# The up-projection of a gated MLP in Winograd form: weight sums added in place by DMAs, other signs and another product order, shifted activation tiles, and attention score products on all 128 rows

## The chip, the cores and the metric

The kernel runs on one core of one Trainium2 chip. The metric is the device time in microseconds (us) of one execution. TensorE is called PE here, VectorE DVE, ScalarE ACT, GpSimd POOL and SyncE SP; PEld is PE's loading of weights (the stationary operand of a matmul), which can run beside a matmul.

## The reference, cut to what matters

One decoder layer on a sequence of 512 tokens, 2048 wide: a mixer of three head groups, a cross-attention, and a gated MLP; all in float32. The change touches two places of it.

```
# the MLP's first half (D_FF = 5504 = 43 tiles of 128)
val, gate = split(h @ w_up, 2)                  # h 512x2048, w_up 2048x11008
g = conv_b + sum(conv_w[i] * shifted(gate, i))  # causal, width 3
out = (silu(g) * val) @ w_down
# groups A (12 heads) and B (8 heads) of the mixer, head width 64
logits = q @ k.T * 64**-0.5 + bias
```

## The kernel before

All activations lie transposed, features on the 128 partitions and tokens along the row. float32 products are made in PE's float32r form: each operand is split into a high part and a rest (`hi` by an ACT copy, `lo` by a DVE subtraction), and a product is three matmuls, high by high, high by low, low by high (`mm3`, lines 351 to 353). Weights come by SP's DMAs into `wraw` tiles (128x1024, 512 KB, five buffers), and are split half by half into `whi` and `wlo` (128x512, five buffers each): line 312 on ACT, line 313 on DVE. PE can so be at most five halves behind the splits.

**Scores (`attend`, lines 491 to 553).** For each of the 20 heads of groups A and B, `qs` holds the high part of the queries in 64 rows and their low part in the other 64, and `kh` holds the high part of the keys twice. So line 516, on 128 rows, gives both products with the high keys. Line 517 adds the high queries by the low keys `kl`, on 64 rows. A head has four such pairs of matmuls, 128, 256, 384 and 512 columns wide, 80 pairs in all. They are issued in the background, between the projection's 512-column products (lines 351 to 353 and 392 to 394), which keep PE filled.

**Sums of activations (`token_sums`, lines 1131 to 1158).** A product of 2x2 blocks is made with seven block products in place of eight. The two blocks of tokens are the first and last 256, the two blocks of outputs are the value and the gate columns of an output tile `f`, and the inner dimension goes in eight pairs of 128-row blocks. For each pair, seven sums or differences of activation blocks are made, split, and kept: 56 tiles `sum` (32 of them in the slots of `xhi` and `xlo`), 128x512, the high part in bytes 0 to 1023 of a row and the low part in bytes 1024 to 2047.

**The products (`up`, lines 1162 to 1235).** For each of the 43 tiles `f`, four weight blocks `b11, b12, b22, b21` are loaded. DVE makes four sums of them in 128x1024 tiles: `t1 = b12 - b11`, `t2 = b22 - t1`, `b22 - b12`, `t2 - b21` (line 1189). The products come in the order 1, 6, 5, 7, 4, 2, 3. Each is eight pairs by three matmuls of 256 columns, 24 in all, from two weight halves; a tile has 168 matmuls, the stage 7,224. Results are combined in PSUM or by DVE and ACT in 256-column pieces, then follow the convolution, the silu, and a store of the tile (`gd`, 256 KB).

A scheduler decides where in each engine's row of instructions a step stands; each engine then runs its row in order. SP's row holds the loads and the stores, POOL's row has nothing in this stage.

Of the kernel before, what the change touches and what calls it, by code (L numbers as in the profile page):

```python
# [40 lines left out]
FT = D_FF // P  # L41
FB = 4
HT = S // 2
# [2 lines left out]
FC = ((0, 5), (5, 10))  # L46
GX_SLOTS = 16
GB_SLOTS = 10
LEVELS = (64, 32, 16, 8, 4, 2, 1)
A_PATTERNS = ((128, 1), (512, 4), (2048, 16))  # L50
REL_BUCKETS = 32
# [5 lines left out]
WR = 5  # L57
# [153 lines left out]
class _Trunk:  # L211
# [77 lines left out]
        return self.gains[:, i * KT + k:i * KT + k + 1]  # L289

    def xslot(self, n=S):
        hi = self.xp.tile([P, n], F32R, name="xhi", tag="xhi", bufs=KT, padded_shape=[P, S])
        lo = self.xp.tile([P, n], F32R, name="xlo", tag="xlo", bufs=KT, padded_shape=[P, S])
        return hi, lo

    def split(self, src, n=S):
# [194 lines left out]
    def attend(self, qf, kf, e, vv, bias_of, head, mix):  # L491
        nc, ab = self.nc, self.ab
        a = slice(DH * e, DH * e + DH)
        o = slice(DH - DH * e, 2 * DH - DH * e)
# [5 lines left out]
        nc.scalar.activation(kh[o], kf[a], AF.Copy)  # L500
# [10 lines left out]
        def scores(t):  # L511
            n = P * (t + 1)
            sc = self.pst("S")
            tt = slice(t * P, n)
            with self.behind():
                nc.tensor.matmul(sc[:, :n], qs[:, tt], kh[:, :n], start=True, stop=False)
                nc.tensor.matmul(sc[:, :n], qs[a, tt], kl[a, :n], start=False, stop=True)
# [613 lines left out]
    def token_sums(self, i, pool, tmp):  # L1131

        nc = self.nc
        y = []
        for e in range(2):
            t = tmp.tile([P, S], F32, name="y%d" % e, tag="y%d" % e, bufs=2)
            nc.scalar.activation(t, self.x1[2 * i + e], AF.Copy, scale=self.gain(2, 2 * i + e))
            y.append(t)
        a11, a21 = y[0][:, :HT], y[0][:, HT:]
        a12, a22 = y[1][:, :HT], y[1][:, HT:]  # L1140
        s = [tmp.tile([P, HT], F32, name="s%d" % n, tag="s%d" % n, bufs=2) for n in range(1, 5)]
        src = {1: a11, 6: s[1], 5: s[0], 7: s[2], 4: a22, 2: a12, 3: s[3]}
        made = {5: (a21, a22, ALU.add), 6: (s[0], a11, ALU.subtract), 7: (a11, a21, ALU.subtract),
                3: (a12, s[1], ALU.subtract)}
        out = {}
        for n, j in enumerate((1, 5, 6, 7, 4, 2, 3)):
            if j in made:
                nc.vector.tensor_tensor(src[j], made[j][0], made[j][1], op=made[j][2])
            slot = 7 * i + n
            if slot < 2 * KT:  # L1150
                tag = ("xhi", "xlo")[slot % 2]
                t = self.xp.tile([P, S], F32R, name=tag, tag=tag, bufs=KT)
# [4 lines left out]
            out[j] = (t[:, :HT], t[:, HT:])  # L1157
        return out


# [1 line left out]
    def up(self):  # L1162
# [9 lines left out]
        def cw(i, f):  # L1172
            return self.conv[:, i * FT + f:i * FT + f + 1]

        def raw(u):
            t = self.wp.tile([P, 1024], F32, name="wraw", tag="wraw", bufs=WR)
            nc.sync.dma_start(out=t, in_=d["w_up"][u])
            return t

        def product(j, w, ps, start, stop):  # L1180
            for h in range(2):
                th, tl = self.split_weights(w[:, h * 512:(h + 1) * 512])
                for k in range(4):
                    i, c = 4 * h + k, slice(k * P, (k + 1) * P)
                    self.mm3(ps, th[:, c], tl[:, c], *self.sums[i][j], start and i == 0, stop and i == NP - 1,
                             more=True)

        def tt(out, a, b, op):
            nc.vector.tensor_tensor(out, a, b, op=op)

        def one(f):
            b11, b12, b22, b21 = [raw(4 * f + i) for i in range(4)]
            pa, pb = self.acc()[:, :HT], self.acc()[:, :HT]
            pc, pd = self.pst("C")[:, :HT], self.pst("D")[:, :HT]
            s1, u2, u3 = [fb.tile([P, HT], F32, name=n, tag=n, bufs=1) for n in ("s1", "u2", "u3")]
            val = fb.tile([P, S], F32, name="val", tag="val", bufs=1)
            gp = gps[f % 2]
            product(1, b11, pa, True, True)
            nc.scalar.activation(s1, pa, AF.Copy)
            t1 = fb.tile([P, 1024], F32, name="t1", tag="t1", bufs=1)  # L1200
            t2 = fb.tile([P, 1024], F32, name="t2", tag="t2", bufs=1)
            tt(t1, b12, b11, ALU.subtract)
            tt(t2, b22, t1, ALU.subtract)
            product(6, t2, pb, True, True)
            tt(u2, pb, s1, ALU.add)
            product(5, t1, pc, True, True)
            if f == 0:
                self.R = self.rms(self.sqs, S, self.con)
            tt(b12, b22, b12, ALU.subtract)
            product(7, b12, pb, False, True)  # L1210
            tt(u3, pb, s1, ALU.add)
            tt(gp[:, 2 + HT:], pc, u3, ALU.add)
            tt(t2, t2, b21, ALU.subtract)
            product(4, t2, pd, True, True)
            tt(val[:, hi], u3, pd, ALU.subtract)
            product(2, b21, pa, False, True)
            nc.scalar.activation(val[:, lo], pa, AF.Copy)
            product(3, b22, pc, False, True)
            tt(gp[:, 2:2 + HT], pc, u2, ALU.add)
            tt(gp[:, 2:], gp[:, 2:], self.R, ALU.mult)  # L1220
# [5 lines left out]
            tt(c, c, val, ALU.mult)  # L1226
            self.gd[f] = self.dr.tile([P, S], F32, name="gd%d" % f)
            nc.sync.dma_start(out=self.gd[f], in_=c)

        self.gd = {}  # L1230
        for f in range(FT):
            one(f)
        es.close()
        self.es_sx.close()
        self.es_fa.close()
# [141 lines left out]

# [13 lines left out]
```

## Time and profile before

| | |
|---|---|
| median of 3 runs | 2430.11 us (2429.5 to 2431.83) |
| the profiled execution | 2430.49 us; span 2428.7 us, so 1.8 us lie around it |
| granted TensorE clock, mean | 0.991 |
| busy, share of the span | PE 98%, PEld 88%, DVE 68%, ACT 47%, POOL 4% |
| 350 to 740 us (groups A and B) | PE 388.82 of 390 us, DVE 260.72, ACT 211.05 |
| 1100 to 1900 us (inside the MLP up stage) | PE 800.00 of 800 us, DVE 704.99, ACT 426.45, 118 GB/s |

The up stage begins at about 1058 us and ends at about 1937 us. In the timeline a row is one instruction: its start, its duration, engine, line, tiles written and read, shape, and in square brackets the idle time before it with what ended it. Matmuls are pipelined, so a row's duration overlaps the next; what PE takes for one is read as the distance of two starts. In the views of waits and of groups the time behind the bar is idle time in front of the instructions and what ended it.

### The profile page before, as it was taken

What the parts mean: (1) busy time and instruction counts of PE and PEld (TensorE: products, weight loads), DVE (VectorE), ACT (ScalarE), POOL (GpSimd) and SP (SyncE); (2) the same over time, 40 slices, a digit from 0 to 9 for tenths busy, and PEclk for the clock granted to TensorE, in tenths of its full rate; (3) what the DMA queues carried; (4) which work ended last, traced back from release to release, by engine and by line L of the source; (5) the groups of instructions that cost most, each with busy time, mean ns of one, the idle gap of its engine ahead of it and who ended that gap; (6) DMA issues with size and microseconds to landing.
All of it is one profiled execution on the core that took longest, in us unless ns stands there. A gap on an engine that the chain in (4) does not pass through costs nothing.

```text
span 2428.7 us, 37893 instructions
## 1 busy us (share of the span) xinstructions
PE 2379.8 (98%) x14514; PEld 2128.5 (88%) x14514; DVE 1660.4 (68%) x3112; ACT 1130.8 (47%) x2165; POOL 88.5 (4%) x91
## 2 busy tenths in 40 slices
PE   9999999999999999889999999999999899999997
PEld 8798987777778888779999999999999888888887
DVE  7726656556786365898888888888888743343336
ACT  6323345455564254665555555555555532232223
POOL 2000000000002000100000000000000000000003
PEclk9999999999999999989999999999999999999999
DMA  6432122222224343123333333333333443243332
GB/s 205 143 100 77 54 97 78 94 79 88 87 70 156 121 143 119 46 76 117 119 121 118 118 118 118 118 118 119 118 119 118 156 141 122 96 156 98 115 102 73
DMA packets 87458, 269.15 MB, mean 111 GB/s; under 512 B 9788, under 2 KB 14540, under 8 KB 87276
## 3 DMA queue, kind: packets, MB, share of 16 engines
q1 hardware_dynamic: 79504, 254.64, 32.5%
q10 hardware_dynamic: 7772, 12.09, 1.5%
q8 instruction: 114, 1.87, 0.3%
q14 instruction: 68, 0.56, 0.1%
HBM read 251.18 MB, written 19.45 MB: 111 GB/s over the span
## 4 chain that ended last, share of the span: by engine, by line
PE 94%; DVE 3%; ACT 1%; POOL 1%; DMA 0%; issue 0%; DVEq 0%; SPq 0%; POOLq 0%; ACTq 0%
PE acc L351 18%; PE acc L353 18%; PE acc L352 18%; PE psC L351 3%; PE psC L353 3%; PE psC L352 3%; PE acc L392 3%; PE acc L394 3%; PE acc L393 3%; PE psD L353 2%; PE psD L352 2%; PE psD L351 2%; PE psV L352 1%; PE psU L352 1%; PE psV L353 1%; PE psU L353 1%
## 5 line engine op out<-in xcount | busy, mean ns | idle before, releaser
L338 DVE TENSOR_TENSOR wlo<-wraw,whi 128x512 fp32r<-128x512 f32 (+2 forms) x496 | 335.8, 681 | 428.6 <-ACT whi L337 421.8
L337 ACT ACTIVATE whi<-wraw 128x512 fp32r<-128x512 f32 (+2 forms) x496 | 304.6, 617 | 655.1 <-PE acc L352 391.7
L351 PE MATMUL acc<-xhi,whi 128*128 128x512 f32 (+1 forms) x1518 | 555.3, 366 | 14.8 <-ACT xhi L1254 8.9
L353 PE MATMUL acc<-xhi,wlo 128*128 128x512 f32 (+1 forms) x1518 | 546.0, 360 | 0.0
L352 PE MATMUL acc<-xlo,whi 128*128 128x512 f32 (+1 forms) x1475 | 533.3, 362 | 0.0
L351 PEld LDWEIGHTS acc<-xhi,whi 128*128 128x128 f32 x1518 | 288.3, 190 | 59.0 <-ACT xhi L1254 9.1
L353 PEld LDWEIGHTS acc<-xhi,wlo 128*128 128x128 f32 x1518 | 288.4, 190 | 42.8 <-issue 0.8
L352 PEld LDWEIGHTS acc<-xlo,whi 128*128 128x128 f32 x1475 | 280.3, 190 | 39.6 <-issue 0.8
L312 ACT ACTIVATE whi<-wraw 128x512 fp32r<-128x512 f32 x344 | 216.7, 631 | 205.2 <-PE acc L352 68.5
L313 DVE TENSOR_TENSOR wlo<-wraw,whi 128x512 fp32r<-128x512 f32 x344 | 232.6, 687 | 37.4 <-ACT whi L312 33.0
L312 ACT ACTIVATE whi<-t 128x512 fp32r<-128x512 f32 x258 | 162.7, 632 | 165.1 <-PE acc L352 98.5
L313 DVE TENSOR_TENSOR wlo<-t,whi 128x512 fp32r<-128x512 f32 x258 | 173.6, 688 | 43.4 <-ACT whi L312 43.1
L351 PE MATMUL acc<-sum,whi 128*128 128x256 f32 x559 | 158.7, 284 | 0.9 <-ACT sum L1155 0.9
L352 PE MATMUL acc<-sum,whi 128*128 128x256 f32 x559 | 158.7, 284 | 0.5 <-DVE sum L1156 0.5
L353 PE MATMUL acc<-sum,wlo 128*128 128x256 f32 x559 | 158.5, 284 | 0.0
L352 PE MATMUL acc<-xhi,whi 128*128 128x256 f32 x430 | 122.1, 284 | 0.0
L392 PE MATMUL acc<-whi,xhi 128*128 128x384 f32 (+2 forms) x320 | 114.8, 359 | 0.6 <-ACT xhi L304 0.5
L394 PE MATMUL acc<-whi,xlo 128*128 128x384 f32 (+2 forms) x320 | 111.9, 350 | 0.5 <-DVE xlo L305 0.4
L393 PE MATMUL acc<-wlo,xhi 128*128 128x384 f32 (+2 forms) x320 | 111.8, 350 | 0.0
L353 PE MATMUL acc<-xlo,wlo 128*128 128x256 f32 x387 | 109.8, 284 | 0.0
L351 PE MATMUL acc<-xlo,whi 128*128 128x256 f32 x387 | 109.8, 284 | 0.0
L351 PEld LDWEIGHTS acc<-sum,whi 128*128 128x128 f32 x559 | 107.7, 193 | 1.1 <-ACT sum L1155 1.1
(368 smaller groups left out, 5267.0 us busy)
## 6 DMA issues: line engine op xcount, KB each, us to landing
wraw<-in_w_up SPq DMA_DIRECT2D x172, 512.0 KB, 3.8
wraw<-in_w_dn SPq DMA_DIRECT2D x80, 512.0 KB, 3.7
wraw<-in_w_o SPq DMA_DIRECT2D x32, 512.0 KB, 3.6
wraw<-in_w_qka SPq DMA_DIRECT2D x24, 512.0 KB, 3.7
gd<-cv SPq DMA_DIRECT2D x43, 256.0 KB, 4.4
graw<-gd SPq DMA_DIRECT2D x43, 256.0 KB, 4.0
wraw<-in_w_qkb SPq DMA_DIRECT2D x16, 512.0 KB, 3.8
xraw<-in_xT SPq DMA_DIRECT2D x15, 512.0 KB, 3.6
```

The costliest lines, as they stand in the source:

```text
L312: nc.scalar.activation(hi, r, AF.Copy)
L313: nc.vector.tensor_tensor(lo, r, hi.bitcast(F32), op=ALU.subtract)
L337: nc.scalar.activation(hi, r, AF.Copy)
L338: nc.vector.tensor_tensor(lo, r, hi.bitcast(F32), op=ALU.subtract)
L351: nc.tensor.matmul(out, lh, rh, start=start, stop=False, skip_group_check=more)
L352: nc.tensor.matmul(out, lh, rl, start=False, stop=False, skip_group_check=more)
L353: last = nc.tensor.matmul(out, ll, rh, start=False, stop=stop, skip_group_check=more)
L392: self.nc.tensor.matmul(o, xh[:, tt], wh, start=(k == 0), stop=False)
L393: self.nc.tensor.matmul(o, xh[:, tt], wl, start=False, stop=False)
L394: self.last = self.nc.tensor.matmul(o, xl[:, tt], wh, start=False, stop=(k == KT - 1))
```

## The change

1. **Weight sums.** DVE's four sums a tile go. Two blocks are loaded into `wraw` (`x` = b11, `y` = b22), b21 into a tile `z`. After each half of `x` or `y` has been split for a product, POOL issues a DMA that loads the same half of another block from HBM and adds it to the tile in place. So `x` serves products 1, 5, 6 and 4 in turn, each with one block more, and `y` serves 3 and 7. That is eight such DMAs of 256 KB a tile, and three loads of 512 KB in place of four.
2. **Signs.** Those DMAs only add, so the sums of activations take other signs, and the results are combined with the signs turned; the gate's minus goes into the multiplication by `R`. A copy of product 5 (`s5`, ACT, 256 columns) is new.
3. **Order.** `one(f)` is a generator: product 1 of tile `f`, then product 7 and the tail of tile `f - 1`, then products 5, 2, 6, 3, 4 of `f`. In tile 0 product 7 of a tile before is missing.
4. **Places of the activations.** The `sum` tiles, and all `xhi` and `xlo` tiles with them, become 528 elements long (2,112 bytes in place of 2,048), and the high part of a sum starts at byte 32 of its tile, the low part at byte 1056.
5. **Scores.** `kl` gets a copy of its 64 rows in the other 64 (one ACT copy of 64x512 a head), and line 517 runs on 128 rows, so it also adds the product of the low parts.
6. The scratch that POOL's DMAs use grows from 1,024 to 2,048 bytes a partition.

```diff
+SHIFT = 8
-        hi = self.xp.tile([P, n], F32R, name="xhi", tag="xhi", bufs=KT, padded_shape=[P, S])
+        hi = self.xp.tile([P, n], F32R, name="xhi", tag="xhi", bufs=KT, padded_shape=[P, S + 16])
...
         nc.vector.tensor_tensor(kl[a], kf[a], kh[a].bitcast(F32), op=ALU.subtract)
+        nc.scalar.activation(kl[o], kl[a].bitcast(F32), AF.Copy)
...
                 nc.tensor.matmul(sc[:, :n], qs[:, tt], kh[:, :n], start=True, stop=False)
-                nc.tensor.matmul(sc[:, :n], qs[a, tt], kl[a, :n], start=False, stop=True)
+                nc.tensor.matmul(sc[:, :n], qs[:, tt], kl[:, :n], start=False, stop=True)
...
-                t = pool.tile([P, S], F32R, name="sum%d" % slot)
-            nc.scalar.activation(t[:, :HT], src[j], AF.Copy)
-            nc.vector.tensor_tensor(t[:, HT:], src[j], t[:, :HT].bitcast(F32), op=ALU.subtract)
+                t = pool.tile([P, S + 16], F32R, name="sum%d" % slot)
+            o = SHIFT
+            th, tl = t[:, o:o + HT], t[:, o + HT:o + S]
+            nc.scalar.activation(th, src[j], AF.Copy)
+            nc.vector.tensor_tensor(tl, src[j], th.bitcast(F32), op=ALU.subtract)
...
-        def product(j, w, ps, start, stop):
+        def product(j, w, ps, start, stop, add=None):
             for h in range(2):
-                th, tl = self.split_weights(w[:, h * 512:(h + 1) * 512])
+                c = slice(h * 512, (h + 1) * 512)
+                th, tl = self.split_weights(w[:, c])
+                if add is not None:
+                    nc.gpsimd.dma_start(out=w[:, c], in_=d["w_up"][add][:, c], accum_op=ALU.add)
...
+            x, y = [load(i, self.wp, "wraw", WR) for i in (u, u + 2)]
+            z = load(u + 3, fb, "z", 1)
...
+            product(1, x, pa, True, True, u + 1)
             nc.scalar.activation(s1, pa, AF.Copy)
-            tt(t1, b12, b11, ALU.subtract)
-            tt(t2, b22, t1, ALU.subtract)
+            yield
+            product(5, x, pc, True, True, u + 2)
+            nc.scalar.activation(s5, pc, AF.Copy)
+            product(2, z, pa, False, True)
+            product(6, x, pb, True, True, u + 3)
+            product(3, y, pc, False, True, u + 1)
+            product(4, x, pd, True, True)
+            yield
+            product(7, y, pb, False, True)
```

DVE's row before, in the middle of the up stage, at the seam of two tiles. `t1` and `t2` are sums of weights, `wlo` the rest of a split, `gp` and `val` pieces of the result.

```order
L1189 TENSOR_TENSOR t2_13959<-wraw_13913,t1_13958 128x1024
L1189 TENSOR_TENSOR u3_13661<-acc_13656,s1_13659 128x256
L313 TENSOR_TENSOR wlo_13868<-wraw_13651,whi_13867 128x512
L1189 TENSOR_TENSOR gp0_9955<-psC_13657,u3_13661 128x256
L313 TENSOR_TENSOR wlo_13884<-wraw_13651,whi_13883 128x512
L1189 TENSOR_TENSOR wraw_13911<-wraw_13913,wraw_13911 128x1024
L1189 TENSOR_TENSOR val_13662<-u3_13661,psD_13658 128x256
```

And now, at the same seam (line numbers are those of the new kernel: 314 is the split, 1197 the helper that was 1189):

```order
L314 TENSOR_TENSOR wlo_14230<-wraw_13917,whi_14229 128x512
L314 TENSOR_TENSOR wlo_14246<-wraw_13917,whi_14245 128x512
L314 TENSOR_TENSOR wlo_14274<-wraw_14179,whi_14273 128x512
L314 TENSOR_TENSOR wlo_14291<-wraw_14179,whi_14290 128x512
L314 TENSOR_TENSOR wlo_14309<-z_14183,whi_14308 128x512
L314 TENSOR_TENSOR wlo_14325<-z_14183,whi_14324 128x512
L1197 TENSOR_TENSOR u3_13928<-s1_13925,acc_13922 128x256
L1197 TENSOR_TENSOR val_13929<-u3_13928,psD_13924 128x256
L1197 TENSOR_TENSOR gp1_9976<-u3_13928,s5_13926 128x256
```

The 128x1024 sums are gone from DVE's row; the splits stand closer together, and the pieces of tile `f - 1` come after splits of tile `f`.

ACT's row now, the splits of one tile from its product 1 on (`wraw_14179` is its `x`, `wraw_13917` the `y` of the tile before, `z_14183` its `z`), with the semaphores that each waits for; those with DMASW count POOL's DMAs.

```order
L313 ACTIVATE whi_14194<-wraw_14179 128x512 [waits DMAHW6_49,PE_49,Activation_49]
L313 ACTIVATE whi_14211<-wraw_14179 128x512 [waits DVE_49,PE_49]
L313 ACTIVATE whi_14229<-wraw_13917 128x512 [waits DMASW6_49,DVE_49,PE_49]
L313 ACTIVATE whi_14245<-wraw_13917 128x512 [waits DMASW7_49,DVE_49,PE_49]
L313 ACTIVATE whi_14273<-wraw_14179 128x512 [waits DMASW0_49,DVE_49,PE_49]
L313 ACTIVATE whi_14290<-wraw_14179 128x512 [waits DMASW1_49,DVE_49,PE_49]
L313 ACTIVATE whi_14308<-z_14183 128x512 [waits DMAHW3_49,DVE_49,PE_49]
L1213 ACTIVATE s1_14189<-acc_14185 128x256 [waits PE_49]
L313 ACTIVATE whi_14324<-z_14183 128x512 [waits DVE_49,PE_49]
L313 ACTIVATE whi_14341<-wraw_14179 128x512 [waits DMASW2_49,DVE_49,PE_49]
```

Between two uses of a half of `x` stand the halves of one other product, and the second use waits for the DMA that was issued after the first.

POOL's row now, the DMAs of one tile; before, POOL had no row in this stage.

```order
L1190 DMA wraw_14179<-in_w_up 128x512 [waits DMAHW6_49,DVE_49]
L1190 DMA wraw_14179<-in_w_up 128x512 [waits DVE_49]
L1190 DMA wraw_14179<-in_w_up 128x512 [waits DMASW0_49,DVE_49]
L1190 DMA wraw_14179<-in_w_up 128x512 [waits DMASW1_49,DVE_49]
L1190 DMA wraw_14179<-in_w_up 128x512 [waits DMASW4_49,DMASW2_49,DVE_49]
L1190 DMA wraw_14179<-in_w_up 128x512 [waits DMASW5_49,DMASW3_49,DVE_49]
L1190 DMA wraw_14181<-in_w_up 128x512 [waits DMAHW1_49,DMASW6_49,DVE_49]
L1190 DMA wraw_14181<-in_w_up 128x512 [waits DMASW7_49,DVE_49]
```

Six go to `x` (three sums by two halves) and two to `y`; each waits for DVE's split of its half, and each for the DMA before it on the same half.

More of the change, by code (lines that the diff above doesn't have):

```diff
@@ L291, in xslot @@
     def xslot(self, n=S):
[L292 to L293 removed]
+        hi = self.xp.tile([P, n], F32R, name="xhi", tag="xhi", bufs=KT, padded_shape=[P, S + 16])
+        lo = self.xp.tile([P, n], F32R, name="xlo", tag="xlo", bufs=KT, padded_shape=[P, S + 16])
         return hi, lo
@@ L1189, in tt, with tmp @@
             nc.vector.tensor_tensor(out, a, b, op=op)
+        def tmp(name, bufs=1, n=HT):
+            return fb.tile([P, n], F32, name=name, tag=name, bufs=bufs)
         def one(f):
-            b11, b12, b22, b21 = [raw(4 * f + i) for i in range(4)]
+            u = 4 * f
+            x, y = [load(i, self.wp, "wraw", WR) for i in (u, u + 2)]
+            z = load(u + 3, fb, "z", 1)
             pa, pb = self.acc()[:, :HT], self.acc()[:, :HT]
             pc, pd = self.pst("C")[:, :HT], self.pst("D")[:, :HT]
-            s1, u2, u3 = [fb.tile([P, HT], F32, name=n, tag=n, bufs=1) for n in ("s1", "u2", "u3")]
@@ L1207, in one @@
+            product(3, y, pc, False, True, u + 1)
+            tt(gp[:, 2:2 + HT], pc, u2, ALU.add)
+            product(4, x, pd, True, True)
             if f == 0:
                 self.R = self.rms(self.sqs, S, self.con)
[L1209 to L1220, printed above, removed]
+            yield
+            product(7, y, pb, False, True)
+            tt(u3, s1, pb, ALU.subtract)
+            tt(val[:, hi], u3, pd, ALU.add)
+            tt(gp[:, 2 + HT:], u3, s5, ALU.add)
+            nc.vector.scalar_tensor_tensor(gp[:, 2:], gp[:, 2:], -1.0, self.R, op0=ALU.mult, op1=ALU.mult)
@@ L1228, in one @@
             nc.sync.dma_start(out=self.gd[f], in_=c)
+            yield
         self.gd = {}
-        for f in range(FT):
-            one(f)
+        g = one(0)
+        next(g)
+        next(g)
+        for f in range(1, FT):
+            n = one(f)
+            next(n)
+            next(g)
+            next(n)
+            g = n
+        next(g)
         es.close()
```

25 lines of the change are left out of this document (11 added, 14 removed).

## The prediction

> **What bounds the kernel now.** I read the chain that ended last first, on the page, then the busy time of each engine in the two stretches that the change touches.
>
> ```profile
> span 2428.7 us, 37893 instructions
> ...
> PE 94%; DVE 3%; ACT 1%; POOL 1%; DMA 0%; issue 0%; DVEq 0%; SPq 0%; POOLq 0%; ACTq 0%
> ```
>
> ```profile
> core 0: us, PE busy (x) PEld busy (x) DVE busy (x) ACT busy (x) POOL busy (x), PEclk, DMA share, GB/s
> 350.00:740.00 390.00, 388.82 (x1763) 301.55 (x1762) 260.72 (x712) 211.05 (x499) 2.17 (x3) 1.00 0.26 83
> 1100.00:1900.00 800.00, 800.00 (x6669) 800.00 (x6669) 704.99 (x1071) 426.45 (x716) 0.00 (x0) 1.00 0.38 118
> ```
>
> PE bounds both. In the up stage it never pauses: 6,669 matmuls in 800 us are 119.96 ns each, and one tile (168 of them) takes 20.15 us. DVE works 88% of that and waits for nothing that PE feels. So only what changes PE's own pace, or what makes PE wait, moves this stage. The pace is read from the distance of starts, here in the up stage (256 columns) and in the down projection (512 columns).
>
> ```profile
> 1403.42 0.28 PE L352 MATMUL psC<-xlo,whi 128*128 128x256 f32 x1
> ...
> 1403.90 0.28 PE L353 MATMUL psC<-sum,wlo 128*128 128x256 f32 x1
> ```
>
> ```profile
> 2007.01 0.39 PE L352 MATMUL acc<-xlo,whi 128*128 128x512 f32 x1
> ...
> 2007.92 0.39 PE L353 MATMUL acc<-xhi,wlo 128*128 128x512 f32 x1
> ```
>
> Four steps each: 0.12 us at 256 columns, 0.2275 at 512. The 256 columns more cost 107 ns, 0.42 ns a column; so at 256 columns about 13 ns of the 120 do not go with the columns. 7,224 times 13 ns are 94 us: that is all that a better pace could bring in this stage.
>
> **The change part by part.**
>
> *Scores.* In the background of the projections stand pairs like these, 512 columns wide (L516 on 128 rows, L517 on 64).
>
> ```profile
> 379.20 0.39 PE L516 MATMUL psS<-kh,qs 128*128 128x512 f32 x1
> 379.51 0.50 PE L517 MATMUL psS<-kl,qs 64*128 64x512 f32 x1
> 379.95 0.50 PE L516 MATMUL psS<-kh,qs 128*128 128x512 f32 x1
> 380.37 0.50 PE L517 MATMUL psS<-kl,qs 64*128 64x512 f32 x1
> 380.80 0.50 PE L351 MATMUL acc<-xhi,whi 128*128 128x512 f32 x1
> 381.14 0.40 PE L352 MATMUL acc<-xlo,whi 128*128 128x512 f32 x1
> ```
>
> From the start of the first L516 to the start of L352 are five matmuls of 512 columns in 1.94 us; at the ordinary 0.2275 they are 1.14. So a pair costs 0.40 us above its columns: some 0.08 before the 64-row product starts, 0.2 behind it, 0.11 behind the next. The same rows with 128 rows in every matmul have none of it (next fence). 80 pairs by 0.40 are 32 us, on PE, which is the bound there. Narrower pairs lose about as much (the penalty does not follow the columns). I count 30, since PE is not quite full in that stretch (388.82 of 390); the ends are 15 (other engines take over half of it back) and 32. A side cost: the new copy, 20 times.
>
> ```profile
> L500 ACT ACTIVATE kh<-kf x20: 618/631/632, 359.4 to 702.3; 64x512 fp32r<-64x512 f32 x20
> ```
>
> A twin of this row, 0.63 us by 20, is 12.6 us of ACT, which is busy 54% there: hidden behind PE; without that cover it would be the 12.6 us.
>
> *Places of the activations.* No run of before has a moving operand 32 bytes off the start of its tile. In the up stage and the down projection every moving tile and every weight tile steps by 2,048 bytes and is read from its start or from 1,024 or 512 bytes on. The nearest rows with tiles that lie otherwise to each other are attention's second products.
>
> ```profile
> 390.94 0.40 PE L549 MATMUL psO<-ptl,vv 128*128 128x512 f32 x1
> 391.18 0.34 PE L548 MATMUL psO<-pth,vv 128*128 128x384 f32 x1
> ...
> 392.80 0.28 PE L548 MATMUL psO<-pth,vv 128*128 128x256 f32 x1
> 392.92 0.28 PE L549 MATMUL psO<-ptl,vv 128*128 128x256 f32 x1
> 393.03 0.22 PE L548 MATMUL psO<-pth,vv 128*128 128x128 f32 x1
> 393.09 0.27 PE L549 MATMUL psO<-ptl,vv 128*128 128x128 f32 x1
> 393.20 0.45 PE L351 MATMUL acc<-xhi,whi 128*128 128x512 f32 x1
> ```
>
> Two products of 256 columns take 0.23 us, 115 ns each, where the up stage has 120; the first of 512 columns takes 0.24 where others have 0.2275; the one of 128 columns, with the weights of the one before, takes 0.06. So the 13 ns are not a fixed price of a matmul, and the exact, unvarying 120 of the up stage looks like two streams, moving columns and the next weights, that hold each other up in step. A shift by 32 bytes can break the step. The ends are 0 and 13 ns a matmul, 0 and 94 us. The rows between give 5 ns; I take the middle, 7 ns (a pace of 113), 7,224 by 7: 51 us. This is the least certain term.
>
> The Trainium skill ("TensorE: Matmul & The Clock Gate", section "Back-to-back issue gap") puts an isolated warm matmul at N/2.4 + 2.5 ns, which is 109 for 256 columns; the trace has 120, and the measurement decides for before. If the shift restored that rule, the term would be 7,224 by 10.8, 78 us.
>
> The longer `xhi` and `xlo` tiles also move the 512-column products of the other stages out of step, three groups on the page:
>
> ```profile
> L351 PE MATMUL acc<-xhi,whi 128*128 128x512 f32 (+1 forms) x1518 | 555.3, 366 | 14.8 <-ACT xhi L1254 8.9
> L353 PE MATMUL acc<-xhi,wlo 128*128 128x512 f32 (+1 forms) x1518 | 546.0, 360 | 0.0
> L352 PE MATMUL acc<-xlo,whi 128*128 128x512 f32 (+1 forms) x1475 | 533.3, 362 | 0.0
> ```
>
> 4,511 of them; the row at 390.94 would charge 12 ns each (54 us), a gain like that above is as open. I take plus 5 us, with minus 20 and plus 30 as ends.
>
> *Sums by DMA.* What DVE is rid of, and what a split costs:
>
> ```profile
> L313 DVE TENSOR_TENSOR wlo<-wraw,whi 128x512 fp32r<-128x512 f32 x316 | 213.7, 687 | 34.7 <-ACT whi L312 30.3
> L312 ACT ACTIVATE whi<-wraw 128x512 fp32r<-128x512 f32 x316 | 199.2, 631 | 189.1 <-PE acc L352 61.8 <-PE psD L352 55.8 <-PE psC L352 31.0
> ...
> L1189 DVE TENSOR_TENSOR t<-wraw 128x1024 f32<-128x1024 f32 x40 | 49.0, 1226 | 1.4
> ```
>
> Four sums of 1.226 us, 4.9 us of DVE a tile, are worth nothing by themselves, since PE never waits; they only give DVE room (17.7 us a tile to 12.8) if PE gets faster. `s5`, the signs and the changed pieces are one ACT copy and equal DVE work: nothing, under PE.
>
> The price is a chain. A half of `x` is split (0.63 + 0.69 = 1.32 us), then POOL's DMA must land (L), then the next split of that half may start. Three such hops, 1 to 5, 5 to 6, 6 to 4, lie in one tile; from product 4 on to product 1 of the next tile there is none, only ACT's two splits (1.3 us). So a tile takes at least 3(L + 1.32) + 1.3 us. At a pace of 113 ns a tile is 18.98 us, and the chain is hidden while L is under 4.57 us; at today's 20.15 while L is under 4.96. Behind POOL's waiting DMA stand only the next ones; behind ACT's waiting split stand the later splits and the pieces, and PE has five halves (7 us) in hand, refilled between product 4 and the next product 1. L is bounded by the transfers of before.
>
> ```profile
> q1 hardware_dynamic: 28453, 93.24, 37.2%
> ...
> wraw<-in_w_up SPq DMA_DIRECT2D x158, 512.0 KB, 3.8
> gd<-cv SPq DMA_DIRECT2D x40, 256.0 KB, 4.4
> ```
>
> ```profile
> ba<-skew ACTq DMA_DIRECT2D x10, 256.0 KB, 2.8
> ba<-cdr ACTq DMA_DIRECT2D x8, 256.0 KB, 3.0
> ```
>
> 256 KB land in 2.8 to 4.4 us, and 256 KB more cost about 0.9 (3.8 against 2.9). An add has also to read the tile, at most 0.9 again: 2.9 to 5.3 us, and POOL's own time to issue it comes on top, which no row of before shows. I take 4.0, between the plain load with that surcharge (3.8) and the store in this very stage (4.4), and so nothing for the chain. Loads: 2.25 MB a tile keep the 16 engines 37.2% of 20.15 us busy, 7.5 us. Now 1.75 MB are plain (5.8 us) and 2 MB are adds, 6.7 us or, read twice, 13.3: 12.5 to 19.1 us, at the upper end just a tile's time. That is a reason for L to be longer, not a bound of its own.
>
> The Trainium skill ("Collectives: The Full Stack", Part 3, on why ReduceScatter is half of AllGather) says that a DMA's add is slow because it reads two sources, not because it adds; no run of before has one. By that rule the upper ends just given (0.9 us, 13.3 us) hold, L is 3.8, and the sum stays as it is.
>
> *Start and end.* On the chain, the first tile's splits wait for two sums:
>
> ```profile
> 1058.10 1.23 DVE t L1189
> ...
> 1059.36 1.24 DVE t L1189
> ```
>
> These 2.5 us go; but in tile 0 nothing stands between products 1 and 5, which shows about one hop less a product, 5.3 - 2.7, some 2.6 us; and the tail behind the last product has two more pieces of 256 columns, 0.8. Together plus 1 us.
>
> *Sum.* Against the profiled execution, 2430.5 us (span plus 1.8; the median of the runs is 0.4 below it): 2430.5 - 30 - 51 + 5 + 1 = 2355.5, called **2356 us**.
>
> **The rivals.**
>
> *Same pace.* The shift brings nothing; the up stage keeps 120 ns. For it: no row of before shows a 32-byte shift, and the page's 512-column row at 390.94 got slower out of step. Against it: 115 ns at 392.80. Then 2430.5 - 30 + 1, with 0 to 5 for the other tiles: about 2403 us.
>
> *The add chain becomes the bound, and the kernel slower.* One mechanism, the DMA behind each split of `x`, in every tile; its price is 3 us a tile for each us of L, 129 us over 43 tiles. From L = 4.57 it eats the gain of the pace (2356 to 2402 at 4.96); the 29 us that scores and ends bring are eaten at 5.2. At L = 6, the upper end with 0.7 us of POOL on top, a tile takes 23.26 us, the stage 134 us more: 2536 us. For it: 4.4 us of the store in this stage, the doubled reading, DMA engines up to full, and a POOL that must issue eight times a tile; nothing in before shows what POOL needs for that. Against it: plain loads of that size at 2.8 to 3.0.
>
> *No effect of the 128 rows* (the penalty belongs to the score's place between other products, not to 64 rows) would add 30 us to any case; the attention rows, which are in the same place without any penalty, speak against it, and I leave it within the ranges.
>
> **How the numbers follow.** The forecast's case (pace between 109 and 117, chain hidden) has 45%, 2328 to 2385. Same pace: 29%, 2385 to 2420. A chain that takes part of the gain (L 4.57 to 4.96): 6%. The chain beyond that: 20%, of which 4 end within 0.2% (about what this measurement can tell from no change, 5 us) and 16 above. So faster 0.80, same 0.04, slower 0.16. The range 2325 to 2450 leaves out some 6% below (more than the whole 13 ns, or gains in the other stages) and 14% above, from L = 5.3 on.
>
> **What would show it.** In the new profile: L517 128 rows high with steps of its columns, and L351 behind it at 0.23; starts of the up stage's matmuls 0.113 apart, or still 0.120; PE 100% busy inside the stage, with ACT's `whi` waiting for PE. The prediction is wrong if ACT's `whi` waits for the adding DMA there and PE has idle time in front of the first matmul of a half; the landing time of those DMAs against 4.57 and 4.96 us then decides by how much.

## The result, and the profile after

The changed kernel takes 2562.09 us (median of 4 runs, 2556.18 to 2565.99) where the kernel before takes 2429.81: a ratio of 1.0542, 95% interval [1.052, 1.0563]. It is slower by 132 us; 2356 was forecast, in a range up to 2450. The profiled execution took 2562.11 us.

On the page of the changed kernel, the span and the chain that ended last, by engine and by line:

```profile
span 2560.0 us, 38641 instructions
...
PE 56%; DMA 26%; issue 9%; DVE 5%; ACT 3%; POOL 1%; ACTq 0%; DVEq 0%; POOLq 0%; SPq 0%
DMA wraw<-in_w_up 25%; PE acc L354 11%; PE acc L352 11%; PE acc L353 11%; PE acc L393 2%; PE acc L395 2%; PE acc L394 2%; DVE wlo L314 2%; PE psV L354 1%; PE psU L354 1%; PE psV L353 1%; PE psV L352 1%; PE psU L353 1%; PE psU L352 1%; ACT whi L313 1%
```

PE had 94% of this chain before. Now a quarter of the span, 640 us, is time in which the work that ends last waits for a DMA into `wraw`. The same two stretches as in the prediction, in the changed kernel:

```profile
core 0: us, PE busy (x) PEld busy (x) DVE busy (x) ACT busy (x) POOL busy (x), PEclk, DMA share, GB/s
350.00:740.00 390.00, 386.92 (x1866) 317.76 (x1865) 276.08 (x740) 235.61 (x549) 9.88 (x10) 1.00 0.30 95
1100.00:1900.00 800.00, 726.73 (x5704) 696.82 (x5704) 461.53 (x780) 346.90 (x645) 240.58 (x272) 0.98 0.80 168
```

Two opposite things stand here. In groups A and B 1,866 matmuls fit where 1,763 did: that stage became faster. In the up stage 5,704 fit where 6,669 did: 140.3 ns each, so a tile of 168 takes 23.56 us in place of 20.15. PE has idle time there, the DMA engines went from 0.38 to 0.80 busy, and even the granted clock is 0.98.

The waits inside the up stage (1150 to 1850 us; in total, times, longest, in us):

```profile
POOL wraw L1190 <- DVE wlo L314: 447.0, 162, 7.0
ACT whi L313 <- DMA wraw<-in_w_up: 296.3, 152, 4.3
DVE wlo L314 <- ACT whi L313: 279.7, 197, 3.8
PEld acc L352 <- ACT whi L313: 46.3, 31, 2.9
```

Read as a chain: PE's weight loads wait for ACT's split, ACT's split waits 152 times for a DMA into `wraw`, 1.95 us each. POOL's wait for DVE is only the other side of the same ring. The same stretch in the view of the DMAs (share of 16 engines; median us from issue to landing):

```profile
q0 software_dynamic: 34128, 62.14, 56.7%
q1 hardware_dynamic: 17133, 54.53, 22.4%
...
wraw<-in_w_up POOLq DMA_DIRECT2D x237, 256.0 KB, 5.3
wraw<-in_w_up SPq DMA_DIRECT2D x60, 512.0 KB, 5.0
```

The adding DMAs (q0) land 5.3 us after their issue starts (POOL's own 0.88 us of issuing is in that), and plain loads that took 3.8 us before now take 5.0. One hop in the timeline, from the second half of product 5 to the second half of product 6:

```profile
1516.24 0.63 ACT L313 ACTIVATE whi<-wraw 128x512 fp32r<-128x512 f32 x1 [0.64 <-DMA wraw<-in_w_up]
...
1516.90 0.69 DVE L314 TENSOR_TENSOR wlo<-wraw,whi 128x512 fp32r<-128x512 f32 x1 [0.57 <-ACT whi L313]
...
1517.95 0.88 POOL L1190 DMA_DIRECT2D wraw<-in_w_up  x1 [0.39 <-DVE wlo L314]
...
1518.93 0.33 SPq L1181 DMA_DIRECT2D z<-in_w_up  x1
...
1523.22 0.28 PE L354 MATMUL acc<-xlo,wlo 128*128 128x256 f32 x1
1525.15 0.63 ACT L313 ACTIVATE whi<-wraw 128x512 fp32r<-128x512 f32 x1 [3.96 <-DMA wraw<-in_w_up]
...
1525.84 0.58 PE L352 MATMUL acc<-xhi,whi 128*128 128x256 f32 x1 [2.33 <-ACT whi L313]
```

DVE ends at 1517.59; POOL starts 0.36 us later and needs 0.88 us to issue; a load of `z` joins on the engines; the next split of that half starts at 1525.15, 7.56 us after DVE's end (a long hop); PE stood still for 2.3 us. This wait cost more than its length, as the granted clock (the third number from the right) shows around it:

```profile
1524.00:1527.00 3.00, 1.16 (x4) 0.94 (x5) 1.17 (x2) 1.85 (x4) 0.14 (x1) 0.74 0.54 87
1527.00:1530.00 3.00, 3.00 (x16) 3.00 (x16) 2.96 (x6) 2.22 (x5) 1.74 (x3) 0.50 0.49 80
1530.00:1533.00 3.00, 3.00 (x19) 3.00 (x19) 1.84 (x4) 1.67 (x3) 0.81 (x1) 0.62 0.86 178
```

Behind the pause PE ran at half clock, 16 matmuls in 3 us where 25 fit.

The scores in the changed kernel, for the pair that the prediction quoted:

```profile
381.92 0.39 PE L518 MATMUL psS<-kh,qs 128*128 128x512 f32 x1
382.14 0.40 PE L519 MATMUL psS<-kl,qs 128*128 128x512 f32 x1
382.38 0.39 PE L518 MATMUL psS<-kh,qs 128*128 128x512 f32 x1
382.61 0.39 PE L519 MATMUL psS<-kl,qs 128*128 128x512 f32 x1
382.83 0.39 PE L352 MATMUL acc<-xhi,whi 128*128 128x512 f32 x1
```

Four matmuls in 0.91 us: the excess of 0.40 us a pair is gone.

### The profile page after: what moved, and what is told of

Same layout as the page of the kernel before. It is cut to its first block, busy times and chain, and to the rows that moved or that the text cites. A ratio compares the mean times of both kernels' runs of the same rounds, so it can differ in the third digit from the quotient of the medians.

```text
span 2560.0 us, 38641 instructions
## 1 busy us (share of the span) xinstructions
PE 2419.0 (94%) x14514; PEld 2140.8 (84%) x14514; DVE 1479.3 (58%) x2940; ACT 1121.6 (44%) x2228; POOL 393.3 (15%) x435
## 4 chain that ended last, share of the span: by engine, by line
PE 56%; DMA 26%; issue 9%; DVE 5%; ACT 3%; POOL 1%; ACTq 0%; DVEq 0%; POOLq 0%; SPq 0%
DMA wraw<-in_w_up 25%; PE acc L354 11%; PE acc L352 11%; PE acc L353 11%; PE acc L393 2%; PE acc L395 2%; PE acc L394 2%; DVE wlo L314 2%; PE psV L354 1%; PE psU L354 1%; PE psV L353 1%; PE psV L352 1%; PE psU L353 1%; PE psU L352 1%; ACT whi L313 1%
## 5 line engine op out<-in xcount | busy, mean ns | idle before, releaser
L314 DVE TENSOR_TENSOR wlo<-wraw,whi 128x512 fp32r<-128x512 f32 x516 | 348.7, 689 | 416.6 <-ACT whi L313 397.5
L354 PE MATMUL acc<-xhi,wlo 128*128 128x512 f32 (+1 forms) x1518 | 554.0, 365 | 8.7 <-DVE wlo L314 8.5
L313 ACT ACTIVATE whi<-wraw 128x512 fp32r<-128x512 f32 x516 | 310.9, 626 | 555.1 <-DMA wraw<-in_w_up 415.4
L1190 POOL DMA_DIRECT2D wraw<-in_w_up x344 | 304.7, 950 | 702.7 <-DVE wlo L314 644.5
L353 PEld LDWEIGHTS acc<-sum,whi 128*128 128x128 f32 x559 | 108.6, 194 | 0.0
L352 PEld LDWEIGHTS acc<-sum,whi 128*128 128x128 f32 x559 | 108.4, 194 | 0.0
```

What stands on the lines that cost most here:

```text
L313: nc.scalar.activation(hi, r, AF.Copy)
L314: nc.vector.tensor_tensor(lo, r, hi.bitcast(F32), op=ALU.subtract)
L352: nc.tensor.matmul(out, lh, rh, start=start, stop=False, skip_group_check=more)
L353: nc.tensor.matmul(out, lh, rl, start=False, stop=False, skip_group_check=more)
L354: last = nc.tensor.matmul(out, ll, rh, start=False, stop=stop, skip_group_check=more)
L1190: nc.gpsimd.dma_start(out=w[:, c], in_=d["w_up"][add][:, c], accum_op=ALU.add)
```

## The experiments

The theory after this result: the ring split, POOL's adding DMA, next split of the same half bounds every tile, because an add takes about 6 us from DVE's end to the next split; the other parts of the change are worth a few us. Rivals: the order of the products or the pieces on DVE and ACT make PE wait; or the longer tiles and the scores are not what they were taken for. First each part by itself.

**Scores alone.** The kernel before, with

```diff
+        nc.scalar.activation(kl[o], kl[a].bitcast(F32), AF.Copy)
...
-                nc.tensor.matmul(sc[:, :n], qs[a, tt], kl[a, :n], start=False, stop=True)
+                nc.tensor.matmul(sc[:, :n], qs[:, tt], kl[:, :n], start=False, stop=True)
```

> The kernel before with the score products alone changed (the copy of kl and 128 rows in the second product). The prediction's step: 80 pairs lose the 0.40 us that they cost above their columns, 30 us, so about 2400 us. Rival: other work takes half of it back, since the up stage of the changed kernel begins only 16 us earlier than before: about 2414 us. Second rival: the 64 rows were not the reason, and it stays at 2430 us. The stretch from 350 to 740 us should hold about 100 more matmuls than before.

Measured: 2404.18 us, ratio 0.9891 [0.9878, 0.9905], some 27 us less. The prediction's step holds: a pair gives 0.34 us (27 us by 80), and what was won is not taken back.

**Shift and longer tiles alone.** The kernel before, with `S + 16` in the four places and `SHIFT = 8` in `token_sums`.

> The kernel before with the longer activation tiles and the shift by 32 bytes alone. The prediction's step: the up stage's pace falls from 120 to 113 ns, 51 us, less 5 us for the 512-column products: about 2384 us. Rival, read from the starts in the changed kernel (256 columns at 118.3 ns in place of 120, 512 columns with xhi and xlo at 231.5 in place of 227.7): 7,224 by 1.7 is 12 us won, some 4,500 by 3.9 is 18 us lost, so about 2436 us, no gain and perhaps a small loss.

Measured: 2431.31 us, ratio 0.9999 [0.999, 1.0008]: nothing. Two effects cancel. The up stage and the down projection of this kernel:

```profile
1100.00:1900.00 800.00, 800.00 (x6774) 800.00 (x6774) 715.17 (x1090) 428.46 (x726) 0.00 (x0) 1.00 0.39 121
1950.00:2350.00 400.00, 400.00 (x1735) 325.37 (x1735) 153.11 (x232) 105.60 (x170) 0.00 (x0) 1.00 0.35 111
```

And the down projection before:

```profile
1950.00:2350.00 400.00, 400.00 (x1767) 331.20 (x1766) 158.76 (x242) 110.66 (x179) 0.00 (x0) 1.00 0.35 115
```

At 256 columns the pace is 118.1 ns in place of 120.0, at 512 it is 230.5 in place of 226.4. The traces show both sides of the balance. From the first to the last matmul on a `sum` tile there are 863.7 us in place of 876.9, 13 us won. But the first of them starts at 1057.9 us in place of 1052.3, and behind the last the kernel takes 506.2 us in place of 499.5, so the other stages lose 12 us.

**The changed kernel without the adds.**

```diff
-                if add is not None:
-                    nc.gpsimd.dma_start(out=w[:, c], in_=d["w_up"][add][:, c], accum_op=ALU.add)
```

> The changed kernel with the adding DMAs left out, so that the products take the unsummed weights (the sums of weights are not made). All else is as in the changed kernel: order, signs, shift, longer tiles, scores, three loads a tile. If the chain through those DMAs is the cause: PE has no idle time in the up stage, a tile takes 168 by 118.3 ns, 19.9 us, and the time is near 2406 us (2430, less 30 for the scores, plus 6 for the shift). Rival, the order of the products and the pieces on DVE and ACT make PE wait: a tile stays over 21 us and the time over 2460 us.

Measured: 2408.97 us in one run; the up stage is full again.

```profile
1100.00:1900.00 800.00, 800.00 (x6759) 800.00 (x6757) 561.31 (x924) 442.01 (x763) 0.00 (x0) 1.00 0.29 94
```

Order, signs, `s5` and the pieces cost PE nothing. All that is lost hangs on eight DMAs a tile.

**The changed kernel with the sums on DVE.**

```diff
-                    nc.gpsimd.dma_start(out=w[:, c], in_=d["w_up"][add][:, c], accum_op=ALU.add)
+                    nc.vector.tensor_tensor(w[:, c], w[:, c], add[:, c], op=ALU.add)
...
-            x, y = [load(i, self.wp, "wraw", WR) for i in (u, u + 2)]
+            x, b, y = [load(i, self.wp, "wraw", WR) for i in (u, u + 1, u + 2)]
```

(and the four `add` arguments name `b`, `y`, `z`, `b`).

> The changed kernel with the four sums of a tile made by DVE in place, half by half (eight additions of 128x512, about 0.69 us each, 5.5 us of DVE a tile), the fourth weight block loaded again into a tile of its own, and everything else as changed. If the DMAs' chain is the only cause, a tile takes 19.9 us and the time is near 2406 us. Rival, DVE at some 18 of 20 us a tile and its waits for ACT delay the splits in this order: PE waits some 0.5 us a product, 3.5 us a tile, and the time is near 2550 us.

Measured: 2406.66 us, ratio 0.99 [0.9886, 0.9913].

```profile
1100.00:1900.00 800.00, 796.62 (x6728) 796.41 (x6726) 727.97 (x1245) 437.64 (x763) 0.00 (x0) 1.00 0.37 120
```

DVE is 91% busy and PE has 99.6%. What PE lacks is not a wait of this stage: the stage ends at 1896 us here, and the window reaches into the pause before the next stage. From 1150 to 1850 us PE is busy for all of the 700 us. With the sums (2406.7) and without any (2409.0) the kernel takes the same: DVE's sums cost nothing, and the same sums by DMA cost 2562.1 - 2406.7 = 155 us.

So the cause lies in the DMAs. What makes one of them take that long? Three runs change one thing each, a fourth leaves the DMAs and gives them time.

**The same DMAs without adding.** Only `accum_op=ALU.add` is taken out.

> The changed kernel with POOL's DMAs overwriting the half instead of adding to it (the sums of weights are not made): the same transfers from HBM, the same queue, the same waits, no reading of the tile. Theory A, the adding makes the landing long: the landing falls from 5.2 us to 4 or less, a tile to 20 to 20.5 us, the time to 2410 to 2430 us, and the software queue's share of the DMA engines to less than half of its 56.7%. Theory B, POOL's issue, the way through its queue and the other loads make it long: the landing stays above 4.8 us and the time above 2520 us.

Measured: 2405.21 us in one run. Its DMAs in 1150 to 1850 us:

```profile
q0 software_dynamic: 22578, 73.99, 34.2%
...
wraw<-in_w_up POOLq DMA_DIRECT2D x282, 256.0 KB, 3.4
```

Theory A by the landing (3.4 us); the time lies 5 us below A's range. The engines' share fell to 34.2%, not below half of 56.7% as A had it, but the tile is shorter too: 8 plain transfers took 34.2% of 19.9 us (5,914 matmuls in these 700 us, 168 a tile), 6.8 us a tile; 8 adds took 56.7% of 23.56, 13.4 us. An add needs twice the engine time of the same bytes loaded. POOL's time for one issue falls as well, from a median of 875 ns to 546.

**Adds alone, without the loads.**

```diff
-            x, y = [load(i, self.wp, "wraw", WR) for i in (u, u + 2)]
-            z = load(u + 3, fb, "z", 1)
+            if f == 0:
+                kept.extend([load(i, self.wp, "wraw", WR) for i in (u, u + 2)])
+                kept.append(load(u + 3, fb, "z", 1))
+            x, y, z = kept
...
+        kept = []
```

> The changed kernel with the adding DMAs kept and the plain loads of weights made for tile 0 alone (x, y and z are kept and added to through all tiles; the other loads are left out, so the products take other weights). It takes 1.5 MB a tile off the DMA engines. Theory C, the adds queue behind the loads on engines that are 80% busy: the landing falls from 5.2 to about 4 us and the tile from 23.56 to 20 us, the time to 2410 to 2430 us. Theory D, an add of 256 KB takes that long by itself: the landing stays above 4.8 us, the tile above 22.5 us and the time above 2510 us.

Measured: 2462.79 us in one run, between the two theories.

```profile
1100.00:1900.00 800.00, 777.63 (x6364) 759.38 (x6363) 514.95 (x870) 389.42 (x719) 266.86 (x302) 1.00 0.67 113
```

```profile
wraw<-in_w_up POOLq DMA_DIRECT2D x265, 256.0 KB, 4.5
```

The tile takes 125.7 ns by 168, 21.12 us. With nothing but adds and the stores of `gd` the landing is 4.5 us, against 3.4 for plain transfers that share the engines with all loads. So the loads account for 0.8 of the 5.3 us and 2.4 us of the tile; the rest is the add's own, and it alone would still miss PE's pace. C and D each hold in part.

**Half the bytes.**

```diff
-                    nc.gpsimd.dma_start(out=w[:, c], in_=d["w_up"][add][:, c], accum_op=ALU.add)
+                    q = slice(h * 512, h * 512 + 256)
+                    nc.gpsimd.dma_start(out=w[:, q], in_=d["w_up"][add][:, q], accum_op=ALU.add)
```

> The changed kernel with each adding DMA cut to the first 256 columns of its half, 128 KB in place of 256 (the sums of weights are made in half of the columns only). Theory E, bytes: what stands above a fixed part shrinks by half; if the fixed part is some 2 us of the 5.2, the landing is 3.6 us, the chain is hidden, and the time is 2406 to 2420 us. Theory F, a fixed price of an adding DMA and of POOL's issue: the landing stays above 4.6 us and the time above 2490 us.

Measured: 2404.14 us in one run.

```profile
wraw<-in_w_up POOLq DMA_DIRECT2D x282, 128.0 KB, 3.5
```

Theory E: 128 KB less takes 1.8 us off the landing, and the chain is hidden, though POOL issues as often. The bytes of the add decide, not the number of its DMAs. A part of the 1.8 us can be the freer engines, since q0's share of them falls from 56.7% to 37.0%.

**The same DMAs in another order.** `one(f)` runs 1 | 5, 2, 3, 6 | 7, 4, so that in the steady state the row is 1 of `f`, 7 and 4 of `f - 1`, 5, 2, 3, 6 of `f`.

```diff
             product(2, z, pa, False, True)
...
+            product(3, y, pc, False, True, u + 1)
             product(6, x, pb, True, True, u + 3)
...
-            product(3, y, pc, False, True, u + 1)
...
-            product(4, x, pd, True, True)
...
             yield
             product(7, y, pb, False, True)
...
+            product(4, x, pd, True, True)
```

> The changed kernel with its products in another order: 1 of tile f, 7 and 4 of tile f - 1, then 5, 2, 3, 6 of f. Nothing is left out. Between two uses of x there are now two other products, so a hop (split, DMA, next split) has three products, 8.5 us, where 1 to 5 and 5 to 6 had two. If the hops are the cause and the DMA engines have room (0.80 busy in a tile of 23.56 us is 18.9 us): a tile takes 19.9 to 20.3 us and the time is 2406 to 2425 us. Rival, the engines are the cause: with 18.9 of 19.9 us the landing grows past 7 us, the tile stays over 21.5 us and the time over 2475 us.

Measured: 2408.09 us, ratio 0.9916 [0.99, 0.9933].

```profile
1100.00:1900.00 800.00, 797.31 (x6725) 796.31 (x6724) 556.39 (x924) 431.40 (x761) 279.70 (x318) 1.00 0.93 198
```

```profile
wraw<-in_w_up POOLq DMA_DIRECT2D x282, 256.0 KB, 5.7
```

This is the plainest evidence. Every DMA of the change is there, each lands even later (5.7 us), and the engines are 93% busy; yet the 154 us are gone, because a hop now has three products (3 by 24 by 118 ns, 8.5 us) where it had two. Not the engines' capacity bound the changed kernel, but a latency with too little work laid over it.

How far does the prediction's formula, tile = 3(L + 1.32) + 1.3, go? Worked back from the tile alone it gives L = 6.10 for the changed kernel and 5.28 for the run without loads. But L can be read in the traces, from the end of DVE's split to the start of ACT's next split of the same half. Over 34 tiles of the up stage (204 hops of `x`) its mean is 5.70 us, and 4.87 without the loads. That is about the landing (5.3 and 4.5) and two hand-overs: 0.36 us from DVE's end to POOL's start and 0.10 from the landing to ACT's start (medians).

What is left of the tile lies in the last term. From the first split of product 4 to the first split of the next product 1 there are 3.0 us in both runs, where the formula has 1.3. The second half of product 4 starts 2.5 us behind the first, as it has a DMA of its own to wait for (1.4 us a tile in the changed kernel). So three hops and a rest make the tile: with these sizes 24.1 and 21.6 us, where 23.6 and 21.1 were measured. At 118.2 ns a tile is 19.86 us, which leaves L some 4.3 us. The plain DMAs (3.4 + 0.46) and the half adds (3.5 + 0.46) lie under that, and both ran at PE's pace; the adds without loads (4.5 + 0.46) lie over it, and did not.

Then the places of the tiles. By the addresses that the program gives its tiles, the place of the moving columns less that of the weights is a multiple of 512 bytes in almost all of these matmuls of the kernel before; the change breaks that.

**Longer tiles, no shift.** The kernel before with `S + 16` alone.

> The kernel before with the longer activation tiles alone (2,112 bytes, no shift). Theory G, any distance between activations and weights that is not a multiple of 512 bytes changes the pace, at 256 columns for the better (120.0 to 118.2 ns) and at 512 for the worse (227.7 to 231.5): the longer tiles alone do it all, and the time is that of the shift, about 2431 us. Theory H, the shift makes the pace and the longer tiles the loss: the up stage stays at 120.0 ns and the time is about 2444 us.

Measured: 2436.82 us in one run; its stages decide.

```profile
1100.00:1900.00 800.00, 800.00 (x6763) 800.00 (x6762) 714.77 (x1088) 431.72 (x726) 0.00 (x0) 1.00 0.38 120
1950.00:2350.00 400.00, 400.00 (x1735) 325.41 (x1734) 153.83 (x233) 107.44 (x173) 0.00 (x0) 1.00 0.35 114
```

118.3 and 230.5 ns, as with the shift: theory G. The steps of 2,112 bytes do it all; the 32 bytes add nothing to it. This one run is 5.5 us slower than the median with the shift; its up stage begins 6.1 us later than in the profile with the shift, and why is not known.

**Weights shifted instead of activations.** The kernel before with the scores, and

```diff
+    def wpair(self, n, o=0):
+        t = self.wp.tile([P, 1152], F32R, name="whl", tag="whl", bufs=WS)
+        return t[:, o:o + n], t[:, o + 512:o + 512 + n]
+
     def split_weights(self, r):
...
-        hi = self.wp.tile([P, n], F32R, name="whi", tag="whi", bufs=WS, padded_shape=[P, 512])
-        lo = self.wp.tile([P, n], F32R, name="wlo", tag="wlo", bufs=WS, padded_shape=[P, 512])
+        hi, lo = self.wpair(n, SHIFT)
```

(elsewhere `wpair` without the shift).

> The kernel before with the 128-row scores, and with the weights' split tiles in place of the activations shifted by 32 bytes, in the up stage alone: both parts of a split lie in one tile of 4,608 bytes, from byte 0 in the other stages and from byte 32 in the up stage. DVE makes the sums as before. Theory G: the up stage runs at about 118.2 ns, 7,224 by 1.8 is 13 us, the other stages keep 227.7, and the scores take 27 off: about 2390 us, a ratio of 0.984. Rival: it is the mixture of distances that the longer tiles make, not the 32 bytes, and one constant distance leaves 120 ns: about 2404 us, a ratio of 0.989.

Measured: 2393.03 us, ratio 0.9843 [0.9829, 0.9856]: theory G.

```profile
1100.00:1900.00 800.00, 793.52 (x6706) 793.31 (x6705) 709.76 (x1081) 429.50 (x723) 0.00 (x0) 1.00 0.38 120
```

The window reaches past the end of the stage, at 1893 us here; the 6.5 us in which PE is idle lie in the pause before the next stage. Inside the stage PE has no idle time:

```profile
1150.00:1850.00 700.00, 700.00 (x5918) 700.00 (x5917) 625.62 (x952) 375.54 (x634) 0.00 (x0) 1.00 0.38 120
```

That is 118.3 ns. One constant distance is enough for the pace, and the other stages, whose weights are not shifted, keep theirs (steps of 0.227 us at 512 columns).

**Only the sums outside `xhi` and `xlo` shifted.** The kernel before with the scores, and in `token_sums`

```diff
-                t = pool.tile([P, S], F32R, name="sum%d" % slot)
...
+                t = pool.tile([P, S + 16], F32R, name="sum%d" % slot)
+            o = SHIFT if slot >= 2 * KT else 0
```

> The kernel before with the 128-row scores, and the shift by 32 bytes in those 24 of the 56 sum tiles alone that do not lie in slots of xhi and xlo (these keep 2,048 bytes). Theory G: 24 of 56 of 13 us, some 6 us, beside the 27 of the scores and no loss in other stages: about 2398 us, a ratio of 0.987. Rival: a matmul's pace hangs on its neighbours too, and the gain is none or the whole 13 us: 2404 or 2391 us.

Measured: 2395.82 us, ratio 0.986 [0.9846, 0.9874]. The interval, 2392.5 to 2399.3, takes in the 2398 of theory G and leaves out 2404; 2391 lies just outside it. The stage itself says more than the time:

```profile
1150.00:1850.00 700.00, 700.00 (x5898) 700.00 (x5897) 623.86 (x949) 375.35 (x632) 0.00 (x0) 1.00 0.38 120
```

That is 118.7 ns, where 24 of 56 at 118.1 and the others at 120.0 would be 119.2. By the starts in the trace, products of the sums that are not shifted run at 118.2 ns in the first five matmuls behind a shifted one, at 119.3 in the next six and at 120.0 from there on. So a matmul's pace hangs on those before it too, as the rival supposed, though neither of its two times came.

**All that helped, sums by DMA.** The order with three products a hop, the scores, the shifted weights, `xhi` and `xlo` at 2,048 bytes.

> All that helped, with the sums by DMA in the order that hides them: 128-row scores, the product order 1, 7, 4, 5, 2, 3, 6 (three products a hop), the weights' split tiles shifted by 32 bytes in the up stage in place of the activations, the activation tiles back at 2,048 bytes. Nothing is left out. If the work taken off DVE is worth nothing because PE never waits for DVE, it is level with the same kernel with DVE's sums: 2390 to 2396 us, a ratio of 0.984. Rival 1, DVE's room also removes the 6.5 us of 800 in which PE still waits there, 8 us over the stage: about 2385 us, 0.981. Rival 2, DMA engines 93% busy cost PE some waits of their own: over 2400 us, 0.988.

Measured: 2394.19 us, ratio 0.985 [0.9836, 0.9863], level with the 0.9843 of the same kernel with DVE's sums: work taken off DVE is worth nothing here, even where the DMAs are hidden. Rival 1 had nothing to win: its 6.5 us are that pause behind the stage. Both kernels beat the kernel before and the changed one.

## Why the prediction was wrong

**The step that failed** is in the part on sums by DMA: "I take 4.0, between the plain load with that surcharge (3.8) and the store in this very stage (4.4), and so nothing for the chain." L was 5.7 us, beyond both of the prediction's thresholds (4.57 and 4.96), so the chain was not hidden; it cost 155 us where nothing had been put down. Most of that L is the landing: 5.3 us from the start of POOL's issue, just the upper end of the 2.9 to 5.3 given. The value was taken from the middle of that range, with nothing for POOL's longer issue (0.88 us, where SP needs 0.33) or for the hand-overs (0.46 us), and from rows taken on engines 37% busy, while the same paragraph put them at up to a whole tile's time.

A second term of the chain was mis-sized: the 1.3 us behind product 4 measured 3.0. With L = 5.7 the formula as written gives a tile of 22.36 us and some 2497 us in all. The rival worked out with L = 6 was a tile of 23.26 us and 2536 us; measured were 23.56 and 2562. That it came so near is luck, an L a little too long beside a rest that was too short. It was given 20%, and the range ended at L = 5.3, below its own worked case.

**The chain's form** held: three hops and a rest make the tile, ACT's `whi` waits for the DMA, and PE is idle ahead of a half's first matmul. The last two had been named as the signs of being wrong.

**The reading of both operands.** By the rule cited from the Trainium skill ("Collectives: The Full Stack", Part 3), an add costs its second read. The trace agrees in size, though no view shows the reads one by one: 13.4 us of the engines a tile for the adds against 6.8 for the same bytes plain, and 0.80 of 23.56 us, 18.8 in all, at the upper end of the 12.5 to 19.1 forecast. As forecast, that is a reason for L to be long and no bound of its own: at 0.93 busy the other order still kept PE's pace.

**Scores**: 30 forecast, 27 measured, mechanism and size right.

**Places of the activations**: 51 us forecast, 13 measured; right in sign, mis-sized fourfold. The 115 ns rested on two starts rounded to 10 ns (0.23 us for two); over all twenty heads the median distance of these starts is 118 ns, which is just the pace that came. The thought of two streams that fall into step is neither shown nor refuted; the return to 120.0 ns some twelve matmuls behind a shifted product is what the runs show of it. The 109 ns that the Trainium skill gives for an isolated matmul ("TensorE: Matmul & The Clock Gate", section "Back-to-back issue gap") was the pace of no run; 118.1 was the best.

**Other stages**: plus 5 forecast with plus 30 as an end, plus 12 measured. The 4,511 products counted there were misread: by shape 1,343 of them have 256 columns, most of them in the up stage, which those groups of the page mix in ("+1 forms"), and 3,168 have 512. The two terms on places together were minus 46 and came out at about 0.

**DVE's relief** at nothing: right, shown twice (2406.7 with DVE's sums and 2409.0 without any; 2393.0 and 2394.2 with all that helped). **Start and end**, plus 1, was too small to be seen.

The sum by the runs: scores -27, places 0, chain +155, against 2430: 2558, where 2562 was measured. The half clock behind long waits is part of the 155: a mean of 0.98 in the stage is some 2% of 1,010 us, 20 us.

## What to carry to other kernels

When work moves from an idle engine into a DMA, count the latency from the last reader's end to the next reader's start, hand-overs included, and lay enough independent work over it before trusting any saving: here the same DMAs cost 155 us with two products a hop and nothing with three. Where an unseen cost's bounds lie on both sides of a threshold, the price beyond the threshold must stand inside the range. And an engine that the bound doesn't wait for gives nothing back when it is relieved.

## What the hardware did that was not expected

- An adding DMA took twice the DMA engines' time of a plain one of the same size (13.4 against 6.8 us for 2 MB), and POOL 875 ns to issue it against 546.
- The granted clock fell to 0.50 for about 5 us after PE had waited 2.3 us. The Trainium skill ("TensorE: Matmul & The Clock Gate", section "Why this matters for your kernels") asks for no idle gaps over about 3 us; this trace has a shorter one that halved the clock. At 1738 us a pause of 1.4 us was followed by 0.52 as well, but from 1100 to 1200 us the clock stayed at 1.00 through four such waits of up to 1.6 us, so the length of one pause doesn't decide it. In the run without loads the up stage's mean stayed at 1.00.
- The places of moving columns and weights change the pace in opposite directions. With almost all distances at multiples of 512 bytes, 256 columns took 120.0 ns and 512 columns 226.4; with activation tiles of 2,112 bytes they took 118.3 and 230.5. A constant 32 bytes on the weights did the same for 256 columns (118.3); for 512 columns no run parts the distance from the tiles' length. Which distances matter, and why, is open.
- A 64-row product between 128-row ones cost about 0.34 us more than the same on 128 rows (27 us over 80 pairs).
